# Loading the tail of the second tile as six transfers of uneven partition counts

## Chip, cores, metric

One core of one Trainium2 chip. The metric is the device time of one execution in microseconds; all runs told here are fast ones (granted TensorE clock 1.00 throughout). "Span" is the profiled part of an execution; for this kernel the time is about 1.7 to 1.8 us longer than the span. A "run" of bytes is the piece of one partition that a transfer moves, and one DMA packet in the trace; a "slab" is a strip of columns over the partitions; a "completion" is the small packet (4 B, recorded with 9 ns in the kernel before) with which an engine reports its share of a transfer, and a transfer has "landed" when all of them have arrived.

## The reference

```python
# x: 1024 x 4096 float32, axis = -1
mean = np.mean(x, axis=axis, keepdims=True)
return ((x - mean) ** 2).astype(np.float32)
```

16.8 MB are read and 16.8 MB written.

## The kernel before

Eight rows of x go to each of 128 partitions, in two tiles of four rows. A tile is thus 128 runs of 64 KB: one transfer in, one out. For each tile ScalarE takes the mean of row 3, VectorE those of rows 0 to 2, and the two share the squares.

```python
x_t = x.rearrange("(p n q) d -> n p (q d)", p=P, q=Q)      # P = 128, Q = 4, D = 4096
...
tiles = []
for i in range(ntiles):                                    # 2 tiles
    x_tile = io.tile([P, Q * D], F32)
    if i:
        nc.vector.memset(x_tile[:, :D], 0.0)               # delays the second load's issue
    nc.sync.dma_start(out=x_tile, in_=x_t[i])
    tiles.append(x_tile)
...
for i in range(ntiles):
    row = [tiles[i][:, q * D:(q + 1) * D] for q in range(Q)]
    m3 = mean_on_act(row[3])                               # ScalarE needs row 3 first
    m0 = mean_on_dve(row[0])                               # VectorE needs row 0 first
    ...                                                    # the rest of means and squares
    nc.sync.dma_start(out=out_t[i], in_=tiles[i])
```

Of the kernel before, what the change touches and what calls it, by code (L numbers as in the profile page):

```python
# [2 lines left out]

os.environ.setdefault("NEURON_RT_ULTRASERVER_MODE", "4")

# [4 lines left out]

F32 = mybir.dt.float32
ACT = mybir.ActivationFunctionType


@with_exitstack
def kernel(
    ctx: ExitStack,
    tc: tile.TileContext,
    x: bass.AP,
    axis: bass.AP,  # L20
    out: bass.AP,
):





    nc = tc.nc

    B, D = x.shape  # L30
    P = nc.NUM_PARTITIONS
    Q = 4
    H = D * 9 // 16
    assert B % (P * Q) == 0
    ntiles = B // (P * Q)
    inv_d = 1.0 / float(D)

    x_t = x.rearrange("(p n q) d -> n p (q d)", p=P, q=Q)
    out_t = out.rearrange("(p n q) d -> n p (q d)", p=P, q=Q)

    io = ctx.enter_context(tc.tile_pool(name="io", bufs=ntiles))
    scratch = ctx.enter_context(tc.tile_pool(name="scratch", bufs=1))
    stats = ctx.enter_context(tc.tile_pool(name="stats", bufs=2 * ntiles * Q))

    tiles = []
    for i in range(ntiles):
        x_tile = io.tile([P, Q * D], F32)
        if i:
            nc.vector.memset(x_tile[:, :D], 0.0)  # L49
        nc.sync.dma_start(out=x_tile, in_=x_t[i])  # L50
        tiles.append(x_tile)

    inorder = tc.keep_in_program_order

    def mean_on_act(row):
        copy = scratch.tile([P, D], F32)
        neg_mean = stats.tile([P, 1], F32)
        nc.scalar.activation(  # L58
            out=copy, in_=row, func=ACT.Identity, scale=-inv_d, accum_out=neg_mean
        )  # L60
        return neg_mean

    def mean_on_dve(row):
        neg_sum = stats.tile([P, 1], F32)
        neg_mean = stats.tile([P, 1], F32)
        inorder(nc.vector.reduce_sum(  # L66
            out=neg_sum, in_=row, axis=mybir.AxisListType.X, negate=True
        ))
        inorder(nc.vector.tensor_scalar_mul(out=neg_mean, in0=neg_sum, scalar1=inv_d))  # L69
        return neg_mean  # L70

    def square_on_act(part, neg_mean):
        inorder(nc.scalar.activation(  # L73
            out=part, in_=part, func=ACT.Square, bias=neg_mean, scale=1.0
        ))

    for i in range(ntiles):
        row = [tiles[i][:, q * D:(q + 1) * D] for q in range(Q)]
        m3 = mean_on_act(row[3])
        m0 = mean_on_dve(row[0])  # L80
        square_on_act(row[3], m3)
        m1 = mean_on_dve(row[1])
        square_on_act(row[0], m0)
        m2 = mean_on_dve(row[2])
        square_on_act(row[1], m1)
        square_on_act(row[2][:, :H], m2)
        back = row[2][:, H:]
        nc.vector.tensor_scalar_add(out=back, in0=back, scalar1=m2)  # L88
        nc.vector.tensor_mul(out=back, in0=back, in1=back)  # L89
        nc.sync.dma_start(out=out_t[i], in_=tiles[i])  # L90


# [1 line left out]
_INS = ['x', 'axis']  # L94
_OUTS = [((1024, 4096), 'float32')]

_NUMBERS = {'axis': -1}


# [26 lines left out]
```

## Time and profile before

| | before |
|---|---|
| time, median (range) | 83.09 us (83.05 to 83.32) |
| span | 81.4 us |
| share of 16 DMA engines' span in which packets ran | 96.0% |
| first and last data packet | 1.74 us, 80.27 us |
| VectorE, ScalarE busy | 45%, 43% |

The lines behind it stand in the prediction. Besides the page and the views, I use the trace's records of single DMA packets (start, duration, size). They do not name the engine, but a packet starts where the previous one of its engine ends (within 7 ns in the kernel before), so I could put them into 16 sequences. Inside a stretch of long packets this is unambiguous.

One more pair of lines of the kernel before will be needed, from its timeline (start us, duration us, engine, line, operation, idle time before it): both engines start the second tile at the same moment, when its load has landed.

```profile
41.99 3.62 ACT L58 ACTIVATE copy<-x_tile 128x4096 f32<-128x4096 f32 x1 [2.58 <-DMA x_tile<-in_x_dram]
41.99 4.42 DVE L66 TENSOR_REDUCE neg_sum<-x_tile 128x1 f32<-128x4096 f32 x1 [2.44 <-DMA x_tile<-in_x_dram]
```

### The profile page before, as it was taken

What the parts mean: (1) busy time and instruction counts of PE and PEld (TensorE: products, weight loads), DVE (VectorE), ACT (ScalarE), POOL (GpSimd) and SP (SyncE); (2) the same over time, 40 slices, a digit from 0 to 9 for tenths busy, and PEclk for the clock granted to TensorE, in tenths of its full rate; (3) what the DMA queues carried; (4) which work ended last, traced back from release to release, by engine and by line L of the source; (5) the groups of instructions that cost most, each with busy time, mean ns of one, the idle gap of its engine ahead of it and who ended that gap; (6) DMA issues with size and microseconds to landing.
All of it is one profiled execution on the core that took longest, in us unless ns stands there. A gap on an engine that the chain in (4) does not pass through costs nothing.

```text
span 81.4 us, 80 instructions
## 1 busy us (share of the span) xinstructions
DVE 36.9 (45%) x17; ACT 34.7 (43%) x13; POOL 0.2 (0%) x4
## 2 busy tenths in 40 slices
DVE  1950000000089999999439999999900000000000
ACT  6000000000089999999339999999800000000000
POOL 0000000000000000000000000000000000000000
DMA  9099975999982999995899996599998299999580
GB/s 515 0 515 515 451 322 258 515 515 515 515 386 129 515 515 515 515 419 225 386 515 515 515 483 290 258 515 515 515 515 386 129 515 515 515 515 419 225 386 0
DMA packets 576, 33.55 MB, mean 412 GB/s; under 512 B 64, under 2 KB 64, under 8 KB 64
## 3 DMA queue, kind: packets, MB, share of 16 engines
q1 hardware_dynamic: 576, 33.55, 96.0%
HBM read 16.78 MB, written 16.78 MB: 412 GB/s over the span
## 4 chain that ended last, share of the span: by engine, by line
DMA 45%; DVE 25%; issue 1%
DMA x_tile<-in_x_dram 45%; DVE neg_sum L66 16%; DVE x_tile L49 4%; DVE x_tile L89 2%; DVE x_tile L88 1%; DVE neg_mean L69 1%
## 5 line engine op out<-in xcount | busy, mean ns | idle before, releaser
L66 DVE TENSOR_REDUCE neg_sum<-x_tile 128x1 f32<-128x4096 f32 x6 | 26.5, 4413 | 20.0 <-DMA x_tile<-in_x_dram 20.0
L73 ACT ACTIVATE x_tile<-x_tile,neg_mean 128x4096 f32<-128x4096 f32 (+1 forms) x8 | 26.0, 3324 | 0.1
L58 ACT ACTIVATE copy<-x_tile 128x4096 f32<-128x4096 f32 x2 | 7.2, 3617 | 23.2 <-DMA x_tile<-in_x_dram 23.2
L49 DVE MEMSET x_tile<- 128x4096 f32 x1 | 3.5, 3472 | 1.7 <-PEq L107 1.7
L89 DVE TENSOR_TENSOR x_tile<-x_tile 128x1792 f32<-128x1792 f32 x2 | 4.1, 2026 | 0.1
L88 DVE TENSOR_SCALAR x_tile<-x_tile,neg_mean 128x1792 f32<-128x1792 f32 x2 | 2.3, 1154 | 0.1
L58 ACT ACT_TABLE_LOAD x1 | 1.3, 1283 | 0.7 <-PEq L107 0.7
L69 DVE TENSOR_SCALAR neg_mean<-neg_sum 128x1 f32<-128x1 f32 x6 | 0.9, 154 | 0.2
L58 ACT ACTIVATION_READ_ACCUMULATOR copy<-x_tile 128x1 f32 x2 | 0.4, 186 | 0.0
L107 POOL MEMSET const-uint8-127<- 128x1 uint8 x1 | 0.1, 103 | 0.0
L107 POOL MEMSET const-bfloat16-1.0<- 128x1 bf16 x1 | 0.1, 102 | 0.0
L107 POOL MEMSET const-float32-1.0<- 128x1 f32 x1 | 0.1, 100 | 0.0
L107 POOL MEMSET const-float32-0.0<- 128x1 f32 x1 | 0.1, 99 | 0.2 <-issue 0.2
## 6 DMA issues: line engine op xcount, KB each, us to landing
x_tile<-in_x_dram SPq DMA_DIRECT2D x2, 29.4
out_dram<-x_tile SPq DMA_DIRECT2D x2, 21.7
```

The lines of the kernel that those rows point to most:

```text
L49: nc.vector.memset(x_tile[:, :D], 0.0)
L58: nc.scalar.activation(out=copy, in_=row, func=ACT.Identity, scale=-inv_d, accum_out=neg_mean)
L66: inorder(nc.vector.reduce_sum(out=neg_sum, in_=row, axis=mybir.AxisListType.X, negate=True))
L69: inorder(nc.vector.tensor_scalar_mul(out=neg_mean, in0=neg_sum, scalar1=inv_d))
L73: inorder(nc.scalar.activation(out=part, in_=part, func=ACT.Square, bias=neg_mean, scale=1.0))
L88: nc.vector.tensor_scalar_add(out=back, in0=back, scalar1=m2)
L89: nc.vector.tensor_mul(out=back, in0=back, in1=back)
L107: nc = _bacc.Bacc("TRN2", target_bir_lowering=False, num_devices=1)
```

## The change

The intent, as the counts show it: a transfer of 128 partitions reports 16 completions, and in the kernel before each of the 16 sequences moves the same 32 runs of 64 KB. In the changed kernel's trace the transfers of 110, 117 and 120 partitions report 11, 13 and 15 completions, those of the remaining 18, 11 and 8 partitions 9, 11 and 8. The last 2304 bytes of every partition's run are loaded in this way, so that some engines get less and the others more. A GpSimd copy from the first tile makes these transfers wait until the first tile has landed (the copy starts at 22.70 us, their issues at 23.39); its result is overwritten by them.

```diff
+    SLABS = ((256, 110), (192, 117), (128, 120))
...
+        lo = Q * D
         if i:
             nc.vector.memset(x_tile[:, :D], 0.0)
-        nc.sync.dma_start(out=x_tile, in_=x_t[i])
+            lo -= sum(width for width, _ in SLABS)
+        nc.sync.dma_start(out=x_tile[:, :lo], in_=x_t[i][:, :lo])
+        if i:
+            nc.gpsimd.tensor_copy(out=x_tile[:, lo:], in_=tiles[0][:, lo - D:Q * D - D])
+            for width, first in SLABS:
+                hi = lo + width
+                for part in (slice(0, first), slice(first, P)):
+                    nc.sync.dma_start(out=x_tile[part, lo:hi], in_=x_t[i][part, lo:hi])
+                lo = hi
```

## The prediction

> **What bounds the kernel now.** I read the page from the top. The engine table and the 40 slices come first:
>
> ```profile
> span 81.4 us, 80 instructions
> DVE 36.9 (45%) x17; ACT 34.7 (43%) x13; POOL 0.2 (0%) x4
> ...
> DMA packets 576, 33.55 MB, mean 412 GB/s; under 512 B 64, under 2 KB 64, under 8 KB 64
> ## 3 DMA queue, kind: packets, MB, share of 16 engines
> q1 hardware_dynamic: 576, 33.55, 96.0%
> ```
>
> No compute engine is busy half the time; the one DMA queue is busy for 96.0% of 16 engines' span. 576 packets are 4 transfers of 128 runs of 64 KB (512) and 64 tiny ones, 16 a transfer, which report completion. The other 4% is 3.3 us, and the start of the span and its end account for it: in the trace's records of single packets the first data packet starts at 1.74 us, the last ends at 80.27 us, and the span ends at 81.4. So I ask next whether a transfer ever waits for its predecessor's work. The queue's own waits and the timeline answer that:
>
> ```profile
> SPq L90 <- DVE x_tile L89: 53.0, 2, 34.1
> SPq L50 <- DVE x_tile L49: 4.0, 1, 4.0
> ```
>
> ```profile
> 0.73 4.75 SPq L50 DMA_DIRECT2D x_tile<-in_x_dram  x2
> ...
> 39.63 0.35 SPq L90 DMA_DIRECT2D out_dram<-x_tile  x1
> 58.94 0.34 SPq L90 DMA_DIRECT2D out_dram<-x_tile  x1
> ```
>
> The columns of the second are start, us and instruction. The issues lie at 0.73, 5.15, 39.63 and 58.94 us. The first issue needed 1.01 us to its first data packet (0.73 to 1.74). So the stores are ready to move data at about 40.64 and 59.95 us. The earliest of the 16 engines finishes the second load at 40.99 and the first store at 60.31. Each store is therefore queued 0.35 us before anyone could go idle: the 53 us of waiting cost nothing. The packets agree: after the first round, each engine starts a packet every 2.414 us without a hole, 31 times.
>
> The page's chain of what ended last goes through compute on the second tile:
>
> ```profile
> DMA x_tile<-in_x_dram 45%; DVE neg_sum L66 16%; DVE x_tile L49 4%; DVE x_tile L89 2%; DVE x_tile L88 1%; DVE neg_mean L69 1%
> ```
>
> I don't follow it, because it steps from the last store to the issue and leaves out that the store stood in line behind the first one. What sets the end is each engine's own queue: start, plus bytes, at 65536 B / 2.414 us = 27.1 B/ns.
>
> One thing is left over: the engines don't end together. At the end of the last store 13 engines end between 79.63 and 79.98 us and three at 80.18, 80.21 and 80.27. This spread of 0.64 us arises in the first packet of each (3.0 to 3.4 us instead of 2.41) and stays the same through all 32 rounds. The last of the three sets the time; the mean of all ends is about 79.9. Perfect balance could therefore win some 0.35 us of 83.09, 0.4%. That is the whole prize.
>
> [...] In this trace the 4-byte completion packets are recorded with 9 ns. Whether a 512 to 1024 byte run costs that much extra, no row of this trace shows.
>
> **The change, part by part.** The memset, both loads' bytes, both stores and all the mathematics remain; the order of instructions on VectorE and ScalarE is the same. What is new:
>
> (a) The second load is cut to 15808 of 16384 elements a partition: 63232 B instead of 65536. Each engine gives up 8 runs x 2304 B = 18432 B, which is 0.679 us at 27.1 B/ns.
>
> (b) Six transfers bring the 2304 bytes back, unevenly. [...] 110 partitions go to 11 engines (10 rows each, 1024 B), 18 to 9 (2 rows); 117 to 13 (9 rows, 768 B), 11 to 11 (1 row); 120 to 15 (8 rows, 512 B), 8 to 8 (1 row). [...]
> - engines 0 to 7: 12 x 1024 + 10 x 768 + 9 x 512 = 24576 B, +6144 against the even share, +0.226 us;
> - engine 8: 24064 B, +0.207 us; 9 and 10: 22016 B, +0.132 us;
> - 11 and 12: 11008 B, -0.273 us; 13 and 14: 4096 B, -0.528 us; 15: nothing, -0.679 us.
> The sum is 294912 B = 128 x 2304, as it must be. So the intent is plain: unload engines 11 to 15, presumably because the late three are among them, and let the rest carry a little more.
>
> (c) Small runs. Engines 0 to 7 process 31 short packets where 8 long ones merely were a bit longer. [...]
>
> (d) The GpSimd copy of 128x576 waits for the first load (22.64 us) and delays the slabs' issue; at six issues of some 0.35 us each (the width of an issue in the timeline) they would be in the queue around 26 us. The main part of the second load keeps the engines occupied until about 40.3. More than 10 us of room, so the copy is free. VectorE's addition on the first tile (36.3 us) also waits for the copy, which will be long past.
>
> (e) Waits. VectorE's first reduction of tile 1 needs only the main part, so it starts some 0.5 to 0.7 us earlier than 41.99. ScalarE begins with row 3, needs all seven transfers and GpSimd, hence starts at about 41.7 to 42.5. It is then ScalarE's chain (41.99 to 58.74 before) which sets the issue of the last store: 58.6 to 59.4 instead of 58.94, data ready at 59.6 to 60.4. Engines 0 to 8 now finish the first store after about 60.6, so for them it stays hidden. Engine 15 may idle up to its saved 0.68 us, which nobody misses.
>
> [...] If all late engines are among 11 to 15, the end is set by the earlier thirteen: between 79.63 and 79.98 before, the latest then at 80.1 to 80.5 against 80.27: -0.15 to +0.25 us. That is the change's best case, nearly a draw, since the added bytes and small packets eat the balance. If one of the three late engines is among 0 to 8, the end moves by the full +0.33 to +0.58 us. The packets' records do not name the engine. Starts come in a sequence over 0.29 us; if that is the engines' order, the late ones are numbers 12, 14 and 15, which fits the design, with number 2 the latest of the low ones (first packet to 5.12 us, so 80.00 at the end). Then the result is 80.00 + 0.33 to 0.58 = 80.33 to 80.58, +0.06 to +0.31. I take about +0.1 us, leaving room for the author's having tuned the counts on measurements.
>
> **Rivals.**
> 1. *The balance works.* The late three are 13 to 15 and short packets cost next to nothing: end near 80.0, time 82.8 us. For it: the staircase 11, 13, 15 hardly arises by chance. Against: +0.226 us of bytes alone takes most of the 0.3 us.
> 2. *Short strided reads are slow.* If the slabs ran at half rate, engines 0 to 7 would take 0.9 us more: 84.2 us, and the last store would be issued late too. Against: rows of the same pitch are read by all engines at full rate before; for: no short run is in the trace.
> 3. *The last store comes too late.* If ScalarE's seven waits or late slabs move its issue beyond 59.3 + 0.35, all engines idle at 60.6, and the time grows one for one, perhaps 83.6. Room before: 0.36 us, after for the heavy engines about as much, because they run later themselves.
> 4. *VectorE's earlier start shortens the end.* It can't: the store queues behind the first store, so an earlier issue is hidden.
>
> **Range and chances.** The middle is 83.09 + 0.1 = 83.2 us. Rival 1 gives the low edge, 82.75; a late heavy engine plus dear short packets, or rival 3, the high edge, 83.75. Two per cent are 1.66 us. Gaining that is impossible in a queue with 33.55 MB at a fixed rate (0.01 is left for what I don't see); losing it takes more than rival 2 (0.03). So 0.96 for within 2%.
>
> **What would show it.** Right: the bytes unchanged at 33.55 MB, packets 576 + 384 short rows + completion packets of 11+9+13+11+15+8 = 67, that is 1027; ScalarE waiting longer than VectorE for the second tile, VectorE starting near 41.3; the last store issued near 59; no stretch without DMA around 60; the span within 0.4 us of 81.4. Wrong: a completion count of 16 for every slab [...], a DMA share that drops at 41 to 43 us (slow short packets), or a hole at 60 us. The time is wrong in kind if it moves by over 0.7 us.

The heavy engines' sum came to +0.33 to +0.58 us: +0.226 us of bytes (6144 B at 27.1 B/ns), and the allowance for 31 short packets and six more completions. The numbers of engines in part (b) had no trace behind them then; the changed kernel's landings showed all six (11, 9, 13, 11, 15 and 8). Numbers such as "engines 0 to 7" are labels, since no record names an engine. The split of bytes takes it that the engines of a smaller count are among those of a larger one. e9 and e10 show this for their pair, where three of the 16 sequences have no short run; for the six transfers of the change it is an assumption.

## The result, and the profile after

The changed kernel takes 83.75 us (83.65 to 83.82, 4 runs) against 83.09 (83.05 to 83.32). The ratio is 1.0073, 95% interval 1.0052 to 1.0094. Ratios here are the mean time of one kernel's fast runs over that of the other's of the same rounds, so not quite the ratio of the medians quoted. It is slower, by less than 2%: the predicted class, at the upper edge of the predicted range, 0.55 us above the predicted middle.

The page of the changed kernel, the same parts as in the prediction, and its chain by lines:

```profile
span 82.0 us, 97 instructions
DVE 36.9 (45%) x17; ACT 34.7 (42%) x13; POOL 0.9 (1%) x5
...
DMA packets 1027, 33.55 MB, mean 409 GB/s; under 512 B 131, under 2 KB 515, under 8 KB 515
## 3 DMA queue, kind: packets, MB, share of 16 engines
q1 hardware_dynamic: 1027, 33.55, 95.7%
...
DMA x_tile<-in_x_dram 21%; ACT x_tile L85 13%; ACT copy L70 5%; ACTq L133 3%; SPq L61 2%; POOLq L133 1%; ACTq L70 0%; POOLq L119 0%
```

Compute has not moved: 36.9 and 34.7 us as before. The bytes are the same; the packets are 1027, which is the number predicted from 11, 9, 13, 11, 15 and 8 engines. The landings of the six transfers confirm each of the six counts. The chain now leads through ScalarE and the slabs' issue; it is as little the bound as VectorE's was before, since the last store still queues behind the first one on most engines. The timeline shows what moved around the second tile:

```profile
22.70 0.66 POOL L57 COPY x_tile<-x_tile 128x576 f32<-128x576 f32 x1 [22.26 <-DMA x_tile<-in_x_dram]
23.39 2.27 SPq L61 DMA_DIRECT2D x_tile<-in_x_dram  x6
...
39.72 20.38 SPq L102 DMA_DIRECT2D out_dram<-x_tile  x2
41.58 4.42 DVE L78 TENSOR_REDUCE neg_sum<-x_tile 128x1 f32<-128x4096 f32 x1 [1.94 <-DMA x_tile<-in_x_dram]
42.95 3.62 ACT L70 ACTIVATE copy<-x_tile 128x4096 f32<-128x4096 f32 x1 [3.53 <-DMA x_tile<-in_x_dram]
```

VectorE starts 0.41 us earlier, ScalarE 0.96 us later, since the last slab has landed only at 42.85. Its data were through at 41.89: the six slabs' landings follow one another at 41.86, 42.08, 42.27, 42.46, 42.66 and 42.85, some 0.2 us apart. e5 shows the same spacing with transfers that carry next to no data (0.18 to 0.20 us), so it does not come from their bytes. The two stores (merged into one row here) are issued at 39.72 and 59.73 us, the second 0.79 us later than before. The queue's own waits say for whom it waited:

```profile
SPq L102 <- DVE x_tile L101: 29.8, 2, 15.8
SPq L133 <- DMA out_dram<-x_tile: 20.8, 1, 20.8
SPq L61 <- POOL x_tile L57: 17.9, 1, 17.9
...
SPq L102 <- DMA x_tile<-in_x_dram: 2.2, 1, 2.2
SPq L102 <- ACT x_tile L85: 1.2, 1, 1.2
```

The 1.2 us for ScalarE's last square (L85) are new: VectorE used to be the later one. With the issue at 59.73, data can flow from 60.69 us. Four engines were through with the first store by then (60.14, 60.33, 60.34 and 60.53) and idled 0.2 to 0.55 us; the other twelve were not. Those four finish between 80.09 and 80.13, the last of all at 80.54: the idling lies beside the path.

Where the span's +0.58 us come from, read off the two traces (us):

| step | before | after | difference |
|---|---|---|---|
| last data packet of the last store ends | 80.27 | 80.54 | +0.28 |
| from there to its last completion reported | 0.34 | 0.44 | +0.10 |
| from there until the issuing engine has passed its last waits | 0.09 | 0.24 | +0.16 |
| from there to the end (clearing semaphores, barriers) | 0.70 | 0.75 | +0.05 |
| span | 81.39 | 81.98 | +0.58 |

Half of the loss is in the data, half comes after the last data packet has ended. In the kernel before, the issuing engine passes one wait after the last landing; in the changed kernel three, at 81.04, 81.10 and 81.16 us, some 0.06 us apart. This is the split of two single executions, of which the first row can differ from one to the next.

### The profile page after: what moved, and what is told of

It reads as the page before. It is cut to its first block, busy times and chain, and to the rows that moved or that the text cites. A ratio compares the mean times of both kernels' runs of the same rounds, so it can differ in the third digit from the quotient of the medians.

```text
span 82.0 us, 97 instructions
## 1 busy us (share of the span) xinstructions
DVE 36.9 (45%) x17; ACT 34.7 (42%) x13; POOL 0.9 (1%) x5
## 2 busy tenths in 40 slices
DMA packets 1027, 33.55 MB, mean 409 GB/s; under 512 B 131, under 2 KB 515, under 8 KB 515
## 3 DMA queue, kind: packets, MB, share of 16 engines
q1 hardware_dynamic: 1027, 33.55, 95.7%
## 4 chain that ended last, share of the span: by engine, by line
issue 27%; DMA 21%; ACT 18%; ACTq 3%; SPq 2%; POOLq 1%
DMA x_tile<-in_x_dram 21%; ACT x_tile L85 13%; ACT copy L70 5%; ACTq L133 3%; SPq L61 2%; POOLq L133 1%; ACTq L70 0%; POOLq L119 0%
## 5 line engine op out<-in xcount | busy, mean ns | idle before, releaser
L85 ACT ACTIVATE x_tile<-x_tile,neg_mean 128x4096 f32<-128x4096 f32 (+1 forms) x8 | 26.0, 3324 | 0.1
L57 POOL COPY x_tile<-x_tile 128x576 f32<-128x576 f32 x1 | 0.7, 662 | 22.3 <-DMA x_tile<-in_x_dram 22.3
```

What stands on the lines that cost most here:

```text
L57: nc.gpsimd.tensor_copy(out=x_tile[:, lo:], in_=tiles[0][:, lo - D:Q * D - D])
L85: inorder(nc.scalar.activation(out=part, in_=part, func=ACT.Square, bias=neg_mean, scale=1.0))
```

## The experiments

My theory: three additive parts, (1) the bytes and short packets on the heavy engines, (2) the number of transfers, which costs after the last data, (3) unevenness itself. Rivals: the late last store, GpSimd's copy, or one of the three alone. All results are correct ones. "Last data" is the end of the last store's last packet; "last waits" is the third row of the table above.

| kernel | transfers in all | short runs per engine | bytes | last data | last waits | time, us | ratio (95%) |
|---|---|---|---|---|---|---|---|
| before | 4 | 0 | even | 80.27 | 0.09 | 83.14 to 83.16 in these rounds | 1 |
| e7 one slab | 5 | 8 | even | 80.18 | 0.08 | 83.23 | 1.0006 (0.9981 to 1.0030) |
| e6 even slabs | 7 | 24 | even | 80.24 | 0.08 | 83.39 | 1.0021 (0.9996 to 1.0045) |
| e11 even slabs ahead | 7 | 24 | even | 80.45 | 0.08 | 83.39 | 1.0025 (1.0006 to 1.0043) |
| e1 six even half-slabs | 10 | 24 | even | 80.31 | 0.24 | 83.67 | 1.0061 (1.0049 to 1.0073) |
| e5 six tiny loads | 10 | 6 | even | 80.56 | 0.19 | 83.67 | 1.0062 (1.0034 to 1.0089) |
| e10 pair, half width | 6 | 0 to 10 | uneven | 80.43 | 0.08 | 83.23 | 1.0014 (0.9997 to 1.0032) |
| e9 pair | 6 | 0 to 10 | uneven | 80.71 | 0.08 | 83.77 | 1.0071 (1.0055 to 1.0088) |
| e4 no copy | 10 | 0 to 31 | uneven | 80.54 | 0.18 | 83.63 | 1.0065 (1.0051 to 1.0079) |
| e12 the change again | 10 | 0 to 31 | uneven | 80.53 | 0.24 | 83.75 | 1.0072 (1.0057 to 1.0086) |
| e3 double width | 10 | 0 to 31 | twice as uneven | 81.11 | 0.24 | 84.35 | 1.0146 (1.0133 to 1.0159) |
| e8 slabs ahead | 10 | 0 to 31 | uneven | 81.22 | 0.18 | 84.35 | 1.0132 (1.0107 to 1.0156) |
| e2 seven loads by partitions | 10 | 0 | even | 127.75 | 0.18 | 130.38 | 1.5682 (1.5655 to 1.5709) |

"Last data" and "last waits" come from one profiled execution, "time" is the median of all. The profiled one was faster than the median in e6 (by 0.20 us), e1 (0.16) and e7 (0.11), and slower in e10 (0.25), e11 (0.09) and e2, so last data of different kernels can't be compared to better than some 0.2 us. One source of the scatter is that the engines' first packets last 2.4 to 3.5 us, differently in each run (3.00 to 3.41 in the kernel before, 2.42 to 3.41 in the changed one). The short runs per engine of the uneven kernels are counted with the prediction's split.

### e1: six even half-slabs

```diff
-                for part in (slice(0, first), slice(first, P)):
+                for part in (slice(0, P // 2), slice(P // 2, P)):
```

> The changed kernel with each slab cut into two halves of 64 partitions: as many transfers (seven for the second tile), the same slab widths, but every engine gets the same bytes and 24 short packets instead of 0 to 31. My theory, a sum of uneven bytes (+0.23 us on the heavy engines), short packets (about 4.7 ns each) and the cost of seven transfers after the last data (about +0.3 us): last data at 80.4 us of the span instead of 80.54, time 83.45 to 83.6, so 0.15 to 0.3 below the changed kernel's 83.75. Rival 'any short packets and many transfers do it': 83.75. Rival 'only the unevenness': 83.1.

Measured 83.67 us, past the top edge of "83.45 to 83.6". So making the bytes even takes off only 0.08 us of 0.66, and the intervals of the two kernels overlap. This contradicts the rival 'only the unevenness' (83.1). It does not contradict the rival 'any short packets and many transfers do it' (83.75), which lies about as near as my own range: 0.51 of the 0.66 us come without any unevenness.

The packets give the price of a short run. They follow one another at 42.3 ns for 1024 B and 33.0 ns for 768 B; at the 27.1 B/ns of the long runs these would be 37.7 and 28.3. Each run thus costs 4.6 to 4.7 ns beyond its bytes: 24 of them 0.11 us, 31 of them 0.15.

### e2: seven transfers without short runs

```diff
-        nc.sync.dma_start(out=x_tile, in_=x_t[i])
+        for p in (0, 16, 32, 48, 64, 80, 96) if i else (0,):
+            n = P - p if p in (0, 96)[i:] else 16
+            nc.sync.dma_start(out=x_tile[p:p + n], in_=x_t[i][p:p + n])
```

> The kernel before with the second tile's load cut by partitions into six transfers of 16 and one of 32, each of whole 64 KB runs: seven transfers, no short packet, equal bytes. My theory: last data as in the kernel before (80.25 to 80.35 us of the span), but the end of the program later by 0.2 to 0.3 us because more transfers have to be waited for and cleared, time 83.3 to 83.4. Rivals 'short packets' or 'unevenness' alone: 83.1, like the kernel before.

Measured 130.38 us. As a test of the time it failed, though its ten transfers have the longer last waits too (0.18 us). It showed something that counts later. Its page and timeline:

```profile
DMA packets 672, 33.56 MB, mean 260 GB/s; under 512 B 160, under 2 KB 160, under 8 KB 160
## 3 DMA queue, kind: packets, MB, share of 16 engines
q1 hardware_dynamic: 672, 33.56, 97.2%
```

```profile
90.02 3.62 ACT L60 ACTIVATE copy<-x_tile 128x4096 f32<-128x4096 f32 x1 [49.29 <-DMA x_tile<-in_x_dram]
```

The engines are "busy" for 97.2% and yet ScalarE gets the second tile at 90.02 instead of 41.99. A busy engine was here not one that moves bytes at its rate: the same 64 KB run took up to 9.5 us instead of 2.42, a factor of 3.9. What causes it this run does not show: the narrow bands change both where the data are written and where they are read.

### e3: twice the unevenness

```diff
-    SLABS = ((256, 110), (192, 117), (128, 120))
+    SLABS = ((512, 110), (384, 117), (256, 120))
```

> The changed kernel with the three slab widths doubled (512, 384, 256): the same seven transfers and the same number of packets, twice the unevenness in bytes (+12288 instead of +6144 on engines 0 to 7). My theory: +0.23 us on the heavy engines, last data about 80.75, time 83.95 to 84.1. Rival 'number of short packets or transfers alone': 83.75 as the changed kernel. If the late last store has become the bound, it is later by about 0.3 and more engines wait for it: time up to 84.2.

Measured 84.35 us, 0.6 us above the changed kernel, where +0.23 of bytes was my theory. Five engines now idle before the last store, issued at 60.17, but again not the last ones. What is new is in the packets: of the 1536-byte runs the fastest took 65 ns, the mean 80 and the slowest 152; of the 2048-byte runs 81, 100 and 266. So there is a cost that is neither bytes nor count. e9 compares uneven with even.

### e4: without GpSimd's copy

```diff
-            nc.gpsimd.tensor_copy(out=x_tile[:, lo:], in_=tiles[0][:, lo - D:Q * D - D])
```

> The changed kernel without GpSimd's copy, so that the six slab transfers are issued right behind the main part at about 5.5 to 7.7 us instead of 23.4 to 25.7. My theory: they stand behind the main part in any case, the copy is free: time 83.65 to 83.85. Rival 'the copy or the late issue costs': 0.2 us or more faster. Rival 'the early issue disturbs the first load': slower.

Measured 83.63 us, 0.02 below the expected range; the intervals of e4 and of the changed kernel overlap. Issued at 5.5 to 7.6 us instead of 23.4 to 25.3, the slabs stand in line all the same. The ratios, 1.0065 against 1.0073 and 1.0072 (e12), are 0.06 us apart, and these runs resolve no better than some 0.2: the copy is free as far as can be told. A small cost can be seen in the traces: with the copy three waits are left after the last landing, without it two (last waits 0.24 and 0.18 us).

### e5: six useless tiny loads

```diff
         nc.sync.dma_start(out=x_tile, in_=x_t[i])
+        if i:
+            for j in range(6):
+                tiny = scratch.tile([16, 16], F32, name=f"tiny{j}")
+                nc.sync.dma_start(out=tiny, in_=x_t[i][:16, :16])
```

> The kernel before with six useless loads of 16 partitions x 64 B issued behind the second tile's load: as many transfers as the changed kernel, no uneven bytes, nothing that compute waits for. In the runs so far the time from the last landing to the end of the span was 0.79 us with 4 transfers and 0.91 to 1.00 with 10. My theory: last data at 80.3 to 80.4 us (six packets of some 7 to 12 ns and six completions), end of span 0.2 us later relative to it, time +0.2 to +0.3, so 83.35 to 83.45. Rival 'the tail is due to late compute or uneven engines': 83.1 to 83.2.

The 7 to 12 ns are those of the tiny packets in the traces: 7 ns for the 24-byte ones, 9 to 12 for all but three of the 4-byte ones in the changed kernel.

Measured 83.67 us, more than expected. Last waits took 0.19 us as expected: waiting for transfers that landed some 38 us before still costs. But the last data came at 80.56 too, 0.2 us beyond my limit: the first packet of the first store took 2.63 us on average instead of 2.42, and many packets of the second load took 2.44 to 2.5. I have no explanation for these that a run supports. The landings give a hint: all data of the second tile's load were through at 41.78 us, but the seven transfers landed at 42.00, 42.19, 42.37, 42.56, 42.75, 42.94 and 43.12, just while the first store's first packets ran. So this run shows the tail, but does not show that the tail is all that six more transfers cost.

### e6 and e7: fewer, even slabs

```diff
-                for part in (slice(0, first), slice(first, P)):
+                for part in (slice(0, P),):
```

e7 has in addition one slab of all 2304 bytes, `SLABS = ((576, P),)`.

> The changed kernel with each slab as one transfer of all 128 partitions: 4 transfers for the second tile instead of 7, 24 short packets on each engine, equal bytes. My theory: +0.11 us of packets, about half of the 0.2 us of tail: 83.35 to 83.5, below the 83.67 of six half-slabs. Rival 'short packets are the cost, not transfers': 83.6 to 83.7 as with half-slabs.

> The last 2304 bytes in one transfer of 128 partitions: 8 runs of 2304 B on each engine, one transfer more than in the kernel before. My theory: 8 x 4.7 ns of packets, 0.03 to 0.1 us of tail: 83.2 to 83.3. Rival 'cutting the load at all costs, because compute on row 3 starts after the slab': 83.5.

Both as expected: 83.39 and 83.23 us. Together with e1 they make a ladder with even bytes. From nothing to one slab: +0.08 us, not resolved. To three slabs with 24 short runs: +0.24 us in all; e6's interval still contains 1, that of e11 with the same slabs just doesn't. To six half-slabs with the same 24 short runs: +0.51 us. The last step adds three transfers and no packet of data, and costs 0.28 us (the intervals, up to 1.0045 and from 1.0049, just don't overlap); in the traces, 0.16 of it is the last waits. With 7 transfers or fewer, the last waits took 0.08 to 0.09 us in every run, with 10 they took 0.18 to 0.24. In these runs it is a step (8 and 9 transfers were not tried): with seven transfers each reports on a semaphore of its own and the last store's is waited for last, with ten two semaphores are used twice (in the changed kernel the last store reports on that of the second load's main part), it is waited for early, and two or three waits are left for after the last landing. That this order is the cause is read from the traces; no kernel was run that removes it.

### e8 and e11: the slabs ahead of the main part

e8 is e4 with the main part of the second tile queued behind its six slabs; e11 is the same with three even slabs.

```diff
-        nc.sync.dma_start(out=x_tile[:, :lo], in_=x_t[i][:, :lo])
+        main = lo
+        if not i:
+            nc.sync.dma_start(out=x_tile, in_=x_t[i])
         if i:
             for width, first in SLABS:
...
+            nc.sync.dma_start(out=x_tile[:, :main], in_=x_t[i][:, :main])
```

> The changed kernel without the copy and with the six slab transfers queued ahead of the second tile's main part: the same bytes and packets on each engine, but VectorE and ScalarE both start when the main part lands, and light engines have their saving earlier. My theory: ScalarE starts at about 42.2 to 42.5 instead of 42.95, the last store is issued by 59.5 instead of 59.73 and fewer engines wait for it; the end is set by the heavy engines all the same: 83.55 to 83.75. Rival 'the late last store is what costs': 83.3 or less.

> Three even slabs of 128 partitions queued ahead of the second tile's main part. With uneven slabs there the main part's first runs took 2.60 to 3.01 us instead of 2.33. Theory [...]: here they take 2.33 to 2.36 us, no short packet is stretched, and the time is 83.3 to 83.5 as with even slabs behind. Rival 'a long run after short ones always restarts slowly': 2.6 us or more again, time 83.8 to 84.0.

e8 went wrong: 84.35 us. ScalarE started at 43.14, not earlier. The packets show it: with the slabs in between, each engine's first run of the main part took 2.60 to 3.01 us instead of 2.33, and the median 512-byte run 43 ns instead of 27. Either a long run restarts slowly after short ones, or uneven counts do it. e11 rules out the first: with even slabs in the same place all first runs took 2.33 us, no short run was stretched, and the time is 83.39, as with even slabs behind. But e11 also has three slab transfers instead of six. For the short runs that is settled elsewhere: none of e1's six even halves was stretched. For the long run behind them it is not: in e5, behind six tiny even transfers, it took 2.63 us instead of 2.42 too. So unevenness as the cause of e8's slow first runs is likely, not shown. These two kernels say nothing of whether the late last store costs, since e8 did not make it earlier; that it doesn't is read from the changed kernel's trace above.

### e9 and e10: one uneven pair

```diff
-    SLABS = ((256, 110), (192, 117), (128, 120))
+    SLABS = ((576, 104),)      # e9;   e10: ((288, 104),)
```

> The last 2304 bytes in two transfers of 104 and 24 partitions[...]: engines 0 to 11 carry 10 runs (+4608 B, +0.17 us), engine 12 its even 8, engines 13 to 15 nothing (-0.68 us). Beside the single even slab (83.23 us) this is unevenness alone, with one transfer and two packets more. My theory: the end is set by engines 0 to 12, 0.1 to 0.25 us later than with the even slab: 83.35 to 83.5. Rival 'relieving the late engines pays': 83.1 or less. Rival 'uneven counts [...] slow everyone': short packets stretched, 83.6 or more.

> The same pair at half the width, 1152 bytes: engines 0 to 11 carry +2304 B (+0.085 us), engines 13 to 15 -0.34 us. It is the gentlest form of the change's intent. My theory: 83.1 to 83.35, indistinguishable from the kernel before (83.15): what balance wins is about what two more transfers cost. Rival 'relieving the late engines pays': 82.9 to 83.05.

e9 against e7 is unevenness nearly by itself: the same 2304 bytes, 128 short runs in both, one transfer more; the last waits are the same 0.08 us. My theory said 83.35 to 83.5; measured 83.77, which is the third rival's number. The two timelines, first e7, then e9:

```profile
41.18 4.42 DVE L78 TENSOR_REDUCE neg_sum<-x_tile 128x1 f32<-128x4096 f32 x1 [1.71 <-DMA x_tile<-in_x_dram]
41.96 3.62 ACT L70 ACTIVATE copy<-x_tile 128x4096 f32<-128x4096 f32 x1 [2.70 <-DMA x_tile<-in_x_dram]
```

```profile
41.69 4.42 DVE L78 TENSOR_REDUCE neg_sum<-x_tile 128x1 f32<-128x4096 f32 x1 [2.07 <-DMA x_tile<-in_x_dram]
42.73 3.62 ACT L70 ACTIVATE copy<-x_tile 128x4096 f32<-128x4096 f32 x1 [3.32 <-DMA x_tile<-in_x_dram]
```

The slab reaches ScalarE 0.77 us later. In e7 all 128 runs of 2304 B took 93 ns, none longer. In e9 they took 93 to 166, 117.5 on average, and the first store's first packets 2.45 to 2.55 us instead of 2.42. My estimate for a heavy engine from these: 0.17 us of bytes, 10 runs x 24.5 ns = 0.25 of stretching, 0.08 on the first store packet, together 0.50. The last data came 0.53 us later than in e7 (80.71 against 80.18).

Was the intent right, are the relieved engines the late ones? In e9 three sequences have no short run (engines 13 to 15 of the expectation); their first packets ended at 5.20, 5.27 and 5.37 us, those of the other thirteen at 4.98 on average, the latest at 5.23. In e10 the three were at 5.10, 5.22 and 5.34. So they do tend to be late, by some 0.2 to 0.3 us; but others are late in some runs as well, and these get the added work.

e10, the gentlest form, is 83.23 us, ratio 1.0014: as expected not told from the kernel before. No version here beats the kernel before.

### e12: the change again

> The changed kernel once more with five rounds, because its four runs leave an interval of 1.0052 to 1.0094, too wide to tell it from six even half-slabs (1.0061). My theory: 83.7 to 83.85, ratio 1.0065 to 1.0085, so at most 0.15 us of unevenness. Rival 'unevenness costs the 0.23 us of its bytes': above 83.9.

83.75 us, ratio 1.0072 (1.0057 to 1.0086), as expected. Against e1's 1.0061 (1.0049 to 1.0073) the net of unevenness in the change is about 0.1 us; the intervals overlap, and 0.25 us is not excluded. Here all 16 first packets ended by 5.20 us, and the last data came at 80.53. In the kernel before each engine's last data ends 74.89 us after its first packet. The last engine was thus delayed by at least 80.53 - 5.20 - 74.89 = 0.44 us.

## Why the prediction was right, and where it fell short

- **What bounds the kernel: right.** Compute is the same to 0.1 us, the time follows the DMA engines' queues and what comes after them. VectorE's earlier start (0.41 us, 0.5 to 0.7 predicted) shortened nothing.
- **The counts of engines: right.** 11, 9, 13, 11, 15 and 8 landings, 1027 packets.
- **Heavy engines +0.33 to +0.58 us: right,** in part by a wide range. At least 0.44 us in e12. The terms: 0.226 of bytes as worked out; 31 short runs 0.15 (at e1's 4.7 ns each); and a term that I did not have, the stretching of runs by uneven counts. It was small in the change: the mean 768-byte run took 39.5 ns instead of 36, the 512-byte run 30.1 instead of 27, the first store packet 2.46 us instead of 2.42; for a heavy engine my estimate is 0.1 us. The store packet's 0.04 us of it need not be unevenness: in e1, with even halves, that packet took 2.44 us on average. In e12 the runs were stretched less (36.9 and 28.3 ns), with the same 83.75 us.
- **The end of data +0.06 to +0.31: right,** +0.28, and +0.26 in e12. The four engines that idled ended early (80.09 to 80.13 us), others became the last (80.54): balance only exchanged who is late.
- **The sum: too small; this is the step that failed.** The sum for the heavy engines, "+0.33 to +0.58 us", was carried over to the time as if the program ended with its last data. What is missing is the term after it: +0.10 us until the last completion is reported, +0.16 of waits passed one after the other, +0.05 of clearing, 0.31 in all against zero. e1 against e6 shows that more transfers alone cost 0.28 us; the same step in the last waits appears in all kernels with ten transfers, with even bytes too. I counted "ScalarE's seven waits", which are beside the path, and not the issuing engine's at the end, which are on it. By the times the transfers weigh more than this split says: with ten transfers and even bytes the loss is already 0.51 us (e1) and 0.52 (e5) of 0.66. That the time still falls on the upper edge of the range, 83.75, is in part luck: the edge was reasoned from a late heavy engine with dear short packets, or from an idle queue; an engine that had not idled was the last, but a run cost 4.7 ns (e1), and the missing tail filled the gap. The prediction's own sign "the span within 0.4 us of 81.4" failed, it was 82.0.
- **The copy is free: right** as far as e4 can tell (0.06 us, not resolved); what its trace shows is one more wait at the end, 0.06 us.
- **ScalarE at 41.7 to 42.5, last store issued by 59.4: too early,** 42.95 and 59.73. The prediction counted the slabs' data but not their landings, which come one after the other, some 0.2 us apart. It idled four engines, none of them the last. Rival 3, all engines idle at 60.6, did not come.
- **Rival 2, slow short reads:** wrong as stated, short runs lost 4.7 ns each and not half their rate. Close to it is what e3, e8 and e9 show, that runs of uneven transfers are stretched (in e9 to 117.5 ns on average from 93).

The waits at the end could have been seen: the view of the queue's waits that the prediction quotes has their line between the two that it shows, and it was left out.

```profile
SPq L121 <- DMA out_dram<-x_tile: 21.2, 2, 19.2
```

Open: why the lag from the last data to its completion is 0.34 us in some traces and 0.41 to 0.45 in others. It was 0.34 and 0.35 in e6 and e7, but 0.44 in e9, e10 and e11 with as few transfers, so 0.10 us of the loss has no shown cause. The traces narrow it: the lag is carried along by each engine. In the changed kernel, e3, e4, e9 and e12 just those engines that had idled before the last store (4, 5, 5, 3 and 5) reported 0.32 to 0.37 us after their last data, and those that had run on 0.42 to 0.47 us (ends and reports taken in order of time). The first store had it already, 0.47 us in the changed kernel against 0.36 before. So it arises before the last store, not with it. Open too is why the parts don't add: unevenness cost 0.54 us from e7 to e9 and 0.08 from e1 to the change. Open last is the mechanism of stretching; no run here shows it. It was the worst in e8, where the transfer queued behind the uneven slabs is a load too (the median 512-byte run took 43 ns instead of 27, in the change 30.1 on average). e1's even halves of 64 partitions show none of it: their runs took 46, 36 and 27 ns, as with 128. But the engines reach these runs up to 0.57 us apart there, so it says little about what happens when they meet.

## What to carry to other kernels

When all DMA engines run without a hole, shifting bytes between them can win at most the way from the mean of their ends to the last (0.38 us here; the prediction had it as some 0.35), and added transfers eat from that (three more cost 0.28 us from e6 to e1): count their landings and the waits at the program's end too, not only bytes and packets. If bytes must be moved between engines, measure the same split with even counts beside it; here 2304 bytes in one even transfer cost 0.08 us (not resolved) and in an uneven pair 0.63. Split loads along the free dimension (e7: 83.23 us), not into narrow bands of neighbouring partitions (e2: 130.38 us).
